# Layer 2's value and output projections as seven products of halves, the output projection in pieces between the next tile's attention steps

## The chip, the cores and the metric

The kernel runs on one core of one Trainium2 chip. The metric is the device time of one execution in microseconds (us). Before the change the median of three runs is 2681.82 us (2680.32 to 2683.97). Times inside an execution come from one profiled execution, whose span is 2682.0 us.

## What is computed

A trunk of two layers over x, 2048 positions of 1024 channels, in float32. Layer 1 is a gated mixer; its output plus x is the residual stream `x1`. Layer 2 is attention over the own chunk of 64 positions and the eight before it:

```python
k, v = jnp.split(rms_norm(x, g_kv) @ w_kv, 2, axis=-1)      # 16 heads of 64
q, z = jnp.split(rms_norm(x, b_norm_g) @ w_qz, 2, axis=-1)
sc = einsum('bqhd,bkhd->bhqk', q * scale, kc) + rel_bias    # 576 keys for each chunk
o  = einsum('bhqk,bkhd->bqhd', softmax(sc), vc)
x  = x + (o * silu(z)) @ w_out
return rms_norm(x, final_g)
```

Every float32 product is made as three products of rounded parts: high x high, high x low, low x high (`mm3`, lines 105 to 108). The low part is what is left of a number after rounding; so each matrix that enters a product is first split, by a copy on ACT (ScalarE) and a subtraction on DVE (VectorE).

## The kernel before

Layer 1 (lines 230 to 957) takes the first half of the time. It already computes its big products block by block as seven products of half-size matrices in place of eight (phases in the order 1, 2, 6, 5, 7, 4, 3, line 499), with sums and differences of quarter matrices on both sides and of the results. Its last stage, called `Po`, is its output projection; it leaves x1 in DRAM and the first 512 rows normalized and transposed in SBUF.

Layer 2 goes over four tiles `t` of 512 positions, and in each tile over eight pairs `p` of heads. For a pair:

- `project(t, p)` (line 988) multiplies the transposed, split input (`xT[t]`) by the weights of Q and of K (`one`, line 975: 24 matmuls of 512 columns each, named `pj`) and, for every second pair, by those of V for two pairs (`proj_v`: four blocks of 128 positions, 24 matmuls of 256 columns each, named `vp`). K and V are split and kept in DRAM for the next tile, which sees this tile's keys as its past.
- `gate(t, p)` makes z of a pair: 24 more `pj` matmuls.
- eight steps `u`: `score` (matmuls `s`; then maximum on DVE, exp on ACT, scaling on POOL, that is GpSimd, line 1135), `flip` (transposes `tp`, a copy on ACT and a subtraction on DVE), and `value` (matmuls `pv`). The scores are two steps ahead of the flips. `value` ends with `og`, the gated output of the pair, kept in SBUF.

While a pair's eight steps run, the next pair's projections are taken in pieces from a generator (`ahead`, `share`, `take`), so that matmuls of the projections fill the waits of attention. In tile 0 each weight block (512 KB) is loaded, scaled by the norm's gain on POOL (line 183), stored as one block (`wk`, `wvv`) and split; in the later tiles the scaled block is loaded again and split again (`load_split`, line 192).

After the last pair of a tile, `b4` (line 1215) does the output projection, `bo`: 192 matmuls of 512 columns, with attention of the next tile only at its end (two scores). Weights are loaded and split there, `og` is split there, the residual is added from DRAM and the final norm is put off to the next tile's steps (`finals`). In the last tile, `b4` is cut in pieces (`tail`) that run beside the last pair.

Transfers are issued from SP, in the order in which its queue has them, and an issue waits in that queue until its data or its buffer is ready. Weight halves lie in eight buffers of 4 KB per partition (tag `T`), fresh blocks in four (tag `raw`). The order of the instructions of each engine is fixed ahead of time: the program's order is their priority, and one that waits by the compiler's plan is passed by later ones.

Of the kernel before, what the change touches and what calls it, by code (L numbers as in the profile page):

```python
# [33 lines left out]
def trunk_kernel(  # L34
# [25 lines left out]
    wk3 = [dram.tile([P, 3, KD * P], F32, name=f"wk3_{p}") for p in range(NPAIR)]  # L60
    wvv = [dram.tile([P, 2, 1024], F32, name=f"wvv{p}") for p in range(NPAIR // 2)]
# [4 lines left out]
    vhd = [  # L66
        [dram.tile([4, P, T], F32, name=f"vhd{t}_{p}") for p in range(NPAIR // 2)]
        for t in range(NT - 1)
    ]


# [38 lines left out]
    def inv_rms(src, name):  # L110

        st = sm.tile([P, 2, 6], F32, tag="st", name=f"st_{name}", bufs=4)
        for c in range(2):
            nc.vector.bn_stats(st[:, c, :], src[:, c * 512 : (c + 1) * 512])
        return inv_rms_of(st, name)

    def inv_rms_of(st, name):
        mv = sm.tile([P, 2], F32, tag="mv", name=f"mv_{name}", bufs=4)
        nc.vector.bn_aggr(mv[:], st[:])
        r = sm.tile([P, 1], F32, tag="rr", name=f"rr_{name}", bufs=4)  # L120
        nc.vector.scalar_tensor_tensor(
            r[:], mv[:, 0:1], mv[:, 0:1], mv[:, 1:2], op0=ALU.mult, op1=ALU.add
        )
        nc.vector.tensor_scalar(r[:], r[:], EPS, None, op0=ALU.add)
        nc.gpsimd.tensor_tensor(r[:], r[:], mhalf[:], op=ALU.pow)
        return r

    def norm_transpose(name, src, pool, tag, bufs, banks=None, junk=None):

        th = sh.tile([P, KD, T], F32R, tag="hh", name=f"hh_{name}")  # L130
        tl = sh.tile([P, KD, T], F32R, tag="hl", name=f"hl_{name}")

        xs = {}

        def norm(b):
            xt = pool.tile([P, D], F32, tag=tag, name=f"bx_{name}_{b}", bufs=bufs)
            nc.sync.dma_start(xt[:], src(b))
            if junk:
                r = sm.tile([P, 1], F32, tag="rr", name=f"rr_{name}_{b}", bufs=4)
                nc.scalar.activation(  # L140
                    junk(f"jk_{name}_{b}"), xt[:], AF.Square, scale=1.0 / 32, accum_out=r[:]
                )
                nc.vector.tensor_scalar(r[:], r[:], EPS, None, op0=ALU.add)
                nc.gpsimd.tensor_tensor(r[:], r[:], mhalf[:], op=ALU.pow)
# [1300 lines left out]
```

## Time and profile before

| what | value |
|---|---|
| median of three runs | 2681.82 us |
| profiled execution, span | 2682.0 us |
| PE busy | 2647.9 us, 99% |
| DVE, ACT, POOL busy | 1920.2, 1275.1, 710.7 us |
| transfers | 615.10 MB on SP's queue, 66.0% of 16 engines' span |
| layer 2 begins at | 1349 us |

The profile names an instruction by its line, its engine, and what it writes and reads (`vp<-wh_bv,hh_b`: the value projection from the high halves of a weight and of the input). PE is the matrix engine, PEld its weight loads, which run beside the matmuls. Busy times of PE count matmuls that overlap in its pipeline. A row of stretches has the stretch, its length, each engine's busy time with its count of instructions, PE's granted clock, the share of the 16 DMA engines that was busy, and GB/s.

### The profile page before, as it was taken

Reading aid. Unit: us, or ns where it says so; the run is one execution under the profiler, and the core shown is the slowest. Engines: PE = TensorE matmul, PEld = TensorE weight load, DVE = VectorE, ACT = ScalarE, POOL = GpSimd, SP = SyncE. Lnnn points to the kernel's source line nnn. Section 1 sums busy time; section 2 is a strip of 40 time slices with the busy share of each in tenths; the row PEclk is TensorE's granted clock in tenths of the full one; section 3 lists DMA queues with packets and bytes.
Section 4 is the critical chain, followed back from the end, with each engine's and each line's share of the span. In section 5 each row is a group of like instructions: output and inputs, shape, how many; then the busy total and the mean of one; then the engine's idle time right before and its main releaser. Section 6 shows DMA issues by size and latency. Waiting matters only on the chain.

```text
span 2682.0 us, 39989 instructions
## 1 busy us (share of the span) xinstructions
PE 2647.9 (99%) x14176; PEld 2272.3 (85%) x14176; DVE 1920.2 (72%) x3187; ACT 1275.1 (48%) x2252; POOL 710.7 (26%) x767
## 2 busy tenths in 40 slices
PE   8999999999999999999999999999999999999997
PEld 7888888888888888888888888888988889888996
DVE  5655677766677568667667666877878777787777
ACT  5422242443434334323255554566655666556663
POOL 3511335152252414014044520211202111021110
PEclk9999999999999999999999999999999999999998
DMA  7898998989888868758476654554455444454331
GB/s 295 316 329 329 345 362 328 328 305 354 328 317 282 313 245 323 279 199 309 152 273 204 203 187 157 181 158 144 158 157 182 146 148 158 142 161 122 115 111 65
DMA packets 212070, 617.65 MB, mean 230 GB/s; under 512 B 24608, under 2 KB 24608, under 8 KB 211872
## 3 DMA queue, kind: packets, MB, share of 16 engines
q1 hardware_dynamic: 211872, 615.10, 66.0%
q8 instruction: 113, 1.85, 0.3%
q14 instruction: 85, 0.70, 0.1%
HBM read 468.21 MB, written 136.31 MB: 225 GB/s over the span
## 4 chain that ended last, share of the span: by engine, by line
PE 90%; DVE 5%; DMA 1%; POOL 1%; issue 1%; ACT 1%; SPq 0%; DVEq 0%; POOLq 0%; ACTq 0%
PE P L108 11%; PE P L107 11%; PE P L106 11%; PE pj L106 6%; PE pj L107 6%; PE pj L108 6%; PE s L1116 4%; PE tp L1155 4%; PE Po L108 4%; PE Po L106 4%; PE Po L107 4%; PE pv L1182 4%; PE vp L108 2%; PE vp L106 2%; PE vp L107 2%; PE bo L106 2%
## 5 line engine op out<-in xcount | busy, mean ns | idle before, releaser
L106 PE MATMUL P<-T,S 128*128 128x512 f32 x1248 | 496.0, 397 | 2.1 <-ACT S L280 2.1
L107 PE MATMUL P<-T,S 128*128 128x512 f32 x1248 | 489.2, 392 | 1.1 <-DVE T L283 1.1
L108 PE MATMUL P<-T,S 128*128 128x512 f32 x1248 | 490.1, 393 | 0.0
L1135 POOL TENSOR_SCALAR pr<-pr,sl 128x640 f32<-128x640 f32 (+4 forms) x256 | 202.2, 790 | 759.2 <-DVE sl L1134 666.4
L1131 ACT ACTIVATE pr<-pr,nm 128x640 f32<-128x640 f32 (+4 forms) x256 | 195.5, 764 | 266.3 <-DVE nm L1124 263.6
L106 PE MATMUL pj<-hh_b,wh_b 128*128 128x512 f32 x768 | 312.0, 406 | 0.2 <-ACT hh_b L166 0.2
L107 PE MATMUL pj<-hl_b,wh_b 128*128 128x512 f32 x768 | 302.7, 394 | 0.0
L108 PE MATMUL pj<-hh_b,wl_b 128*128 128x512 f32 x768 | 301.6, 393 | 0.0
L108 PEld LDWEIGHTS P<-T,S 128*128 128x128 f32 x1248 | 235.4, 189 | 50.3
L106 PEld LDWEIGHTS P<-T,S 128*128 128x128 f32 x1248 | 235.8, 189 | 47.0 <-ACT S L280 2.3
L107 PEld LDWEIGHTS P<-T,S 128*128 128x128 f32 x1248 | 235.7, 189 | 47.0 <-DVE T L283 1.3
L1159 DVE TENSOR_TENSOR pt<-tp,pt 128x640 fp32r<-128x640 f32 (+4 forms) x256 | 188.8, 737 | 59.1 <-ACT pt L1158 56.5
L1124 DVE CUSTOM_DVE_ANT_0 pr<-s,bias 128x640 f32<-128x640 f32 (+4 forms) x256 | 188.2, 735 | 46.4 <-PE s L1116 42.6
L108 PEld LDWEIGHTS pj<-hh_b,wl_b 128*128 128x128 f32 x768 | 144.5, 188 | 33.3
L1155 PE MATMUL tp<-ident,pr 128*128 128x128 f32 x1120 | 165.0, 273 | 6.2 <-DVE pt L1159 5.0
L1158 ACT CAST pt<-tp 128x640 fp32r<-128x640 f32 (+4 forms) x256 | 159.2, 622 | 22.3 <-PE tp L1155 17.8
L1155 PEld LDWEIGHTS tp<-ident,pr 128*128 128x128 f32 x1120 | 134.7, 140 | 33.9 <-POOL pt L1148 4.8
L106 PEld LDWEIGHTS pj<-hh_b,wh_b 128*128 128x128 f32 x768 | 144.9, 189 | 19.2 <-ACT hh_b L166 0.5
L107 PEld LDWEIGHTS pj<-hl_b,wh_b 128*128 128x128 f32 x768 | 145.3, 189 | 17.4
L106 PE MATMUL vp<-wh_bv,hh_b 128*128 128x256 f32 x512 | 148.8, 291 | 0.9 <-ACT hh_b L166 0.9
L108 PE MATMUL vp<-wh_bv,hl_b 128*128 128x256 f32 x512 | 146.0, 285 | 0.2
L107 PE MATMUL vp<-wl_bv,hh_b 128*128 128x256 f32 x512 | 145.5, 284 | 0.0
(212 smaller groups left out, 6027.3 us busy)
## 6 DMA issues: line engine op xcount, KB each, us to landing
S<-hsd SPq DMA_DIRECT2D x288, 512.0 KB, 5.4
rw<-in_w_a SPq DMA_DIRECT2D x108, 512.0 KB, 6.2
raw_b<-wk SPq DMA_DIRECT2D x75, 512.0 KB, 3.6
A<-ytd SPq DMA_DIRECT2D x72, 512.0 KB, 5.2
hsd<-S SPq DMA_DIRECT2D x56, 512.0 KB, 4.0
bias<-reld SPq DMA_DIRECT2D x64, 320.0 KB, 3.4
raw_bo<-in_wb_out SPq DMA_DIRECT2D x36, 512.0 KB, 4.1
va<-vd SPq DMA_DIRECT2D x32, 512.0 KB, 5.2
```

The source lines that it names most:

```text
L106: mm(ps, lh, rh, start=first, stop=False)
L107: mm(ps, lh, rl, start=False, stop=False)
L108: mm(ps, ll, rh, start=False, stop=last)
L1116: mm(ps[:, sg, :w], q[:, qb * P : (qb + 1) * P], kx[:, koff + sg * w : koff + (sg + 1) * w], start=i == 0, stop=i == 1,)
L1124: nc.vector.tensor_tensor_reduce(out=pr[:, c0:].rearrange("p (a b) -> p a b", a=nseg), in0=ps[:, :nseg, :w], in1=bias[:, c0:].rearrange("p ...
L1131: nc.scalar.activation(pr[:, c0:], pr[:, c0:], AF.Exp, scale=-1.0, bias=nm[:], accum_out=sl[:])
L1135: nc.gpsimd.tensor_scalar(pr[:, c0:], pr[:, c0:], sl[:], 1.0, op0=ALU.mult, op1=ALU.mult)
L1155: tpose(tp[:, b, :], pr[:, b * P : (b + 1) * P], ident[:])
L1158: nc.scalar.copy(oh, tp[:, b0:5, :])
L1159: nc.vector.tensor_tensor(pt[:, 1, b0 + qq : 5 + qq, cs], tp[:, b0:5, :], oh.bitcast(F32), op=ALU.subtract)
L1182: mm(po[:, 0, :], keys(i), pt[:, j, i, :], start=(t == 0 and j == 0 and i == blocks[0]), stop=(j == 1 and i == blocks[-1]),)
```

## The change

Four things are changed, all in layer 2 or in what prepares it.

1. **Values.** The whole value projection of a tile is done at once (`v_all`) as seven products of halves: rows in blocks of 128 (even and odd blocks are the two halves), the inner dimension in two halves of 512, the columns in two halves of 512. Each product is 2 x 4 x 3 = 24 matmuls of 512 columns. The weights' sums (`v_sums`) are made in layer 1's last stage and kept in DRAM (`vwf`); in tile 0 they are loaded, split, and both halves stored (`vws`); later tiles load the halves. The sums of the input run on POOL. The results are split and stored in DRAM, and `values` loads, for each pair, the keys' values of the last and of this tile.
2. **Outputs.** The gated output goes to DRAM (`ogd`). `o_all(t)` is the output projection in the same form, with weight sums made beside pairs 1 to 4 of tile 0 (`o_sums`). It runs in pieces of three matmuls beside tile t + 1's attention, by the table `SHARE`; the last tile's runs partly beside its last pair and then to the end. The finished rows go to DRAM (`x2d`) and come back for the final norm; the sums of squares are made on ACT.
3. **Weights of Q, K and z.** Tile 0 splits them and stores both halves (two stores of 512 KB in place of one); later tiles load the two halves and don't split.
4. **Order.** The next tile's norm, transposes, first projections and values stand beside the last pair of a tile (76 steps), and its first two scores are issued there too. With V done at once, `gate` is run for each pair.

The core of the diff:

```diff
+    def split_w(raw, name, keep):
+        wh, wl = w_tile(f"wh_{name}"), w_tile(f"wl_{name}")
         nc.scalar.copy(wh[:], raw[:])
         nc.vector.tensor_tensor(wl[:], raw[:], wh[:].bitcast(F32), op=ALU.subtract)
+        for i, w in enumerate((wh, wl)):
+            nc.sync.dma_start(keep[:, i, :], w[:].bitcast(F32))
         return wh, wl
+    def kept_w(keep, name):
+        out = [w_tile(f"w{i}_{name}") for i in "hl"]
+        for i, w in enumerate(out):
+            nc.sync.dma_start(w[:].bitcast(F32), keep[:, i, :])
+        return out
+    def v_right(t):
+        def right(ph):
+            out = []
+            for q in range(2):
+                name = f"bv{t}_{ph}_{q}"
+                if t:
+                    out.append(kept_w(vws[ph, q], name))
+                    continue
+                raw = sh.tile([P, 1024], F32, tag="T", name=f"raw_{name}", bufs=8)
+                nc.sync.dma_start(raw[:], vwf[ph, q][:])
+                out.append(split_w(raw, name, vws[ph, q]))
+            return out
+        return right
...
+        def values(t, p):
+            v = vtl[t, p] = sb.tile([P, 8, 256], F32R, tag="V", name=f"V{t}_{p}", bufs=2)
+            for i, tt in enumerate((t - 1, t)):
+                if tt >= 0:
+                    nc.sync.dma_start(v[:, i * TB : (i + 1) * TB, :].bitcast(F32), vhd[tt][:, p])
...
+        PHS = (1, 7, 2, 6, 5, 4, 3)
+        def strassen(name, right, left, evict):
+            for ph in PHS:
+                rt = right(ph)
+                lt = left(ph)
+                for jp in range(2):
+                    views = lt(jp)
+                    ps = pmm.tile([P, 512], F32, tag="mm", name=f"{name}_{ph}_{jp}")
+                    for k in range(4):
+                        hi, lo = rt[k // 2]
+                        c = slice((k % 2) * 512, (k % 2) * 512 + 512)
+                        mm3(ps[:], *views[k], hi[:, c], lo[:, c], k == 0, k == 3)
+                        if k < 3:
+                            yield
+                    evict(ph, jp, ps[:])
+                    yield
...
+            def left(ph):
+                if ph == 1:
+                    for jp in range(2):
+                        a11, a12, a21, a22 = (raw(jp, r, h) for r in range(2) for h in range(2))
+                        tg(a22, a21, a22, op=add)
+                        tg(a21, a11, a21, op=sub)
+                        tg(a11, a22, a11, op=sub)
+                        tg(a12, a12, a11, op=sub)
...
+        def o_sums(u):
+            q, i = divmod(u, 2)
+            cs = slice(i * 512, i * 512 + 512)
+            w = {}
+            for rc in ((0, 0), (0, 1), (1, 1), (1, 0)):
+                w[rc] = c_tile(f"wo{u}_{rc[0]}{rc[1]}")
+                nc.sync.dma_start(w[rc][:], wb_out[rc[0], rc[1], q][:, cs])
+            def keep(ph, src):
+                hi, lo = (half_tile("S", f"so{u}_{ph}{x_}", 6, F32R) for x_ in "hl")
+                nc.scalar.copy(hi[:], src)
+                tv(lo[:], src, hi[:].bitcast(F32), op=sub)
+                for n, y_ in enumerate((hi, lo)):
+                    nc.sync.dma_start(ows[ph, q][:, n, cs], y_[:].bitcast(F32))
...
-                ogt[t, p] = og
+                o4 = og[:].rearrange("p (j r s) -> p r j s", j=2, r=2)
+                for r_ in range(2):
+                    nc.sync.dma_start(ogd[t][:, r_, p], o4[:, r_])
...
+        SHARE = {1: (0, 9, 9, 9, 9, 10, 10, 0), 2: (0, 9, 9, 9, 9, 10, 10, 0)}
+        SHARE[3] = (0, 3, 4, 4, 4, 4, 4, 33)
...
         def ahead(t, p):
             if p + 1 < NPAIR:
                 yield from project(t, p + 1)
+                values(t, p + 1)
+                if p == 0:
+                    yield from gate(t, 0)
+                yield from gate(t, p + 1)
             elif t + 1 < NT:
-                yield from project(t + 1, 0, b1(t + 1, sb, "bx", 2))
-            else:
-                yield from tail
+                norm, block = b1(t + 1, bank4, junk)
+                for b in range(TB):
+                    norm(b)
+                for b in range(TB):
+                    block(b)
+                    yield
+                yield from project(t + 1, 0)
+                yield from v_all(t + 1)
+                values(t + 1, 0)
+            if t:
+                yield from some(outs[t - 1], SHARE[t][p])
+            if t + 1 == NT and p + 1 == NPAIR:
+                yield from some(outs[t], 16)
```

`w_tile` is a buffer of the eight with tag `T`. `tg` is a sum on POOL, `tv` one on DVE.

646 lines of the change are left out of this document (361 added, 285 removed).

## The prediction

> **What bounds the kernel now.** I read the page's busy shares first, then the stretches by tile of layer 2, then the transfers.
>
> ```profile
> span 2682.0 us, 39989 instructions
> PE 2647.9 (99%) x14176; PEld 2272.3 (85%) x14176; DVE 1920.2 (72%) x3187; ACT 1275.1 (48%) x2252; POOL 710.7 (26%) x767
> ...
> q1 hardware_dynamic: 211872, 615.10, 66.0%
> ```
>
> The matrix engine is busy 99% of the span, so at first sight every matmul taken away is time won. The profiled span of 2682.0 us and the median of the runs, 2681.82 us, are the same to 0.01%, so I sum against the span and add nothing for what lies around it. The transfers move 615.10 MB in 66.0% of the span: 347 GB/s for each full share of the 16 engines. That second row is what the change leans on. Five stretches say more: one of layer 1 in which the transfers are full, then the four tiles of layer 2 (columns: length; busy time of PE, PEld, DVE, ACT and POOL; clock; share of the DMA engines; GB/s).
>
> ```profile
> 325.00:375.00 50.00, 50.00 (x233) 41.79 (x232) 36.38 (x57) 19.62 (x32) 11.64 (x8) 1.00 1.02 406
> 1349.00:1669.00 320.00, 312.45 (x1800) 273.02 (x1801) 217.17 (x488) 170.56 (x382) 113.59 (x164) 0.98 0.63 210
> 1669.00:2009.00 340.00, 338.76 (x2081) 301.72 (x2080) 270.18 (x525) 202.44 (x361) 64.42 (x104) 1.00 0.51 158
> 2009.00:2349.00 340.00, 338.57 (x2081) 301.50 (x2080) 269.98 (x525) 202.26 (x361) 64.46 (x104) 1.00 0.49 154
> 2349.00:2682.00 333.00, 318.87 (x1916) 281.55 (x1914) 260.26 (x509) 191.06 (x343) 63.12 (x99) 0.98 0.37 116
> ```
>
> The most that the transfers carry for long is 406 GB/s, with a share of 1.02, and PE lost nothing under it. Tile 0 of layer 2 moves 210 GB/s over 320 us, which is 67.2 MB; tiles 1 and 2 move 53 MB each. So before the change PE is the bound in every tile, and DVE, at 270 of 340 us, is the next engine.
>
> **PE's part of the change.** A busy time of PE counts overlapping instructions, so I take the distance between starts. The first pair of rows bounds 33 steps of the value projection (256 columns each), the second 18 steps of the output projection (512 columns).
>
> ```profile
> 1365.20 0.28 PE L108 MATMUL vp<-wh_bv,hl_b 128*128 128x256 f32 x1
> ...
> 1369.14 0.28 PE L108 MATMUL vp<-wh_bv,hl_b 128*128 128x256 f32 x1
> ```
>
> ```profile
> 1647.81 0.39 PE L106 MATMUL bo<-wh_bo,oh 128*128 128x512 f32 x1
> ...
> 1651.88 0.39 PE L106 MATMUL bo<-wh_bo,oh 128*128 128x512 f32 x1
> ```
>
> That is 3.94/33 = 0.119 us for a narrow matmul and 4.07/18 = 0.226 us for a wide one. The counts come from the stretches of the value projection (PE's count is the first one in brackets), those of the Q, K and gate projections in tiles 0 and 1, and the groups of the output projection.
>
> ```profile
> 1349.00:1669.00 320.00, 65.97 (x480) 61.93 (x480) 11.43 (x40) 10.43 (x40) 0.98 0.63 210
> 1669.00:2009.00 340.00, 53.01 (x384) 48.76 (x384) 8.91 (x32) 8.40 (x32) 1.00 0.51 158
> 2009.00:2349.00 340.00, 53.01 (x384) 48.77 (x384) 8.90 (x32) 8.39 (x32) 1.00 0.49 154
> 2349.00:2682.00 333.00, 38.88 (x288) 36.45 (x288) 6.79 (x24) 6.35 (x24) 0.98 0.37 116
> ```
>
> ```profile
> 1349.00:1669.00 320.00, 162.94 (x624) 112.68 (x624) 30.01 (x44) 25.78 (x44) 0.98 0.63 210
> 1669.00:2009.00 340.00, 150.79 (x576) 102.94 (x576) 27.45 (x40) 23.41 (x40) 1.00 0.51 158
> ```
>
> ```profile
> L106 PE MATMUL bo<-wh_bo,oh 128*128 128x512 f32 x256 | 101.3, 396 | 3.1 <-ACT oh L1232 3.1
> L107 PE MATMUL bo<-wl_bo,oh 128*128 128x512 f32 x256 | 100.9, 394 | 0.0
> L108 PE MATMUL bo<-wh_bo,ol 128*128 128x512 f32 x256 | 100.8, 395 | 0.7 <-DVE ol L1233 0.7
> ```
>
> Values: 480+384+384+288 = 1536 narrow matmuls, 183 us. Seven products of halves need, per tile, 7 x 2 row pairs x 4 blocks x 3 terms = 168 wide ones; four tiles 672, 152 us. Outputs: 768 wide ones, 174 us, become 672, 152 us. So the arithmetic is worth 31 + 22 = 53 us (2.0%), and no more: the value projection is not cut to 7/8 of wide work but gains also from its width.
>
> By tile (320, 340, 340, 333 us now): tile 0 loses 480 narrow (57 us) and 192 wide (43 us), and gets two value projections, its own and tile 1's, 336 wide (76 us): 296 us of PE work. Tiles 1 and 2 lose 46 and 43 and get 38 for the next tile's values and 38 for the last tile's outputs: 327 us each. Tile 3 loses 34 and 43 and gets two output projections, 76: 332 us.
>
> **The transfers' part.** The split weights are now kept as two halves, high and low, and each product has its own weight blocks. The sizes:
>
> ```profile
> bias<-reld SPq DMA_DIRECT2D x64, 320.0 KB, 3.4
> ...
> raw_bv<-wvv SPq DMA_DIRECT2D x26, 512.0 KB, 3.7
> raw_b<-in_w_kqz SPq DMA_DIRECT2D x24, 512.0 KB, 4.6
> wk<-raw_b SPq DMA_DIRECT2D x24, 512.0 KB, 2.9
> khd<-K SPq DMA_DIRECT2D x48, 256.0 KB, 3.9
> vhd<-V SPq DMA_DIRECT2D x48, 256.0 KB, 2.8
> ...
> Qh<-Qh SPq DMA_DIRECT2D x64, 128.0 KB, 2.2
> ```
>
> A 512 KB block is 0.524 MB. Tile 0 after the change, in order, beside PE's work (0.226 us a matmul; attention is what tile 0 keeps besides, (296 - 76 - 624 x 0.226)/8 = 9.9 us a pair of heads):
>
> a) First projections and the whole value projection. Two weights, each loaded once and stored twice: 3.1 MB. Fourteen value blocks loaded and 28 stored: 22.0 MB. Values stored 4.2 MB, small ones (K, Q copies, bias) 1.7 MB. Together 31 MB; PE has 216 matmuls and two scores, 51 us.
>
> b) Pair 0: four weights of 1.57 MB and 2.5 MB for K, Q, bias, values and the gated output: 8.8 MB against 32 us of PE.
>
> c) Pairs 1 to 4: three weights (4.7 MB), 2.5 MB as before, and a quarter of the output weights' sums, 1.05 MB in and 3.67 MB out: 11.9 MB each against 26 us (72 matmuls and attention). Four: 47.6 MB, 104 us.
>
> d) Pairs 5 and 6: 7.2 MB each against 26 us.
>
> e) Pair 7, with tile 1's values: 28 kept blocks 14.7 MB, two kept weights 2.1, values stored and reread 5.2, x 2.1, small ones 2.5: 26.6 MB against 59 us.
>
> That is 128 MB, nearly double the 67.2 MB of now; PE's 296 us would need 430 GB/s, above the 406 of the fullest stretch. In a, c and e the transfers end last. Three ends for the rate: 406 GB/s (that stretch), 347 (the whole run's per full share), and, if the queue never runs empty so that only the tile's total counts, 128/0.406 = 315 us. Loads here wait for one of eight weight buffers, which stay taken until the stores out of them have landed, so the queue will not always be full; a, c and e are nevertheless nearest to the full stretch. I take 385 GB/s: a 81, b 32, c 124, d 52, e 69, together **358 us, +38**. At 406 it is 76+32+117+52+66 = 343 (+23); at 347 it is 89+32+137+52+77 = 387 (+67).
>
> The Trainium skill, page "DMA: Bandwidth & Descriptors", section Specifications, puts the HBM limit of a core at about 358 GB/s and the fabric's ceiling at 435. By the first, tile 0 would take 378 us and the kernel about 2735 us, by the second 326 and 2683. The 406 GB/s over 50 us above already exceeds the first figure, so I don't use it.
>
> The issuing queue is no end of its own: an issue takes about a third of a microsecond,
>
> ```profile
> 1354.93 0.32 SPq L189 DMA_DIRECT2D wk<-raw_b  x1
> ```
>
> and tile 0 has some 300, about 100 us of 358. But it works in order, so a store that waits for its split holds the loads issued behind it. What else is moved, the next tile's first two scores out of the old output projection into the last pair, keeps its count and lies beside the values' matmuls: 0, and about 2 us if the pair is already waiting, which is inside the bounds below.
>
> **Tiles 1 to 3.** There the 24 weights come as ready halves, so 24 splits each leave ACT and DVE; DVE falls below its 270 us although the new sums and evictions come in, and is no bound. A tile moves about 100 MB: 53 now, 12.6 more for halves, 10 more each for value and output weights, the rest for values read by pair, the gated output's and the residual's round trips. Over 327 us that is 306 GB/s. Only the last pair is short: 26.6 MB, 69 us, against 48.8 + (327 - 76 - 130)/8 = 64 us of PE. With 2 us for the four norm blocks which now stand at that pair's head, tiles 1 and 2 take 334 us: **-6 each**. Bounds -13 (all hidden) and 0 (at 347 GB/s).
>
> Tile 3 has no value projection. The output's last products now need the gated output back from DRAM:
>
> ```profile
> 2636.89 0.70 DVE og L1206
> 2637.62 0.52 ACT oh L1232
> 2638.18 0.80 PE bo L106
> 2638.98 0.43 PE bo L107
> ```
>
> Now PE goes on 1.3 us after the gated output is begun. After, a store (2.8 us in the row of vhd) and a load (3.7 in that of wvv) stand between, 6.5 us, and nothing else is left to do. Bounds: 0, if the two early products of that tile are still running, and 10, if the clock stays low longer. -1 for PE and +6.5: **+5**.
>
> The extra value-weight sums in layer 1's last stage (about 9 MB more transfers over 300 us, beside matmuls) I put at +2, between 0 and 6. The sums on POOL (0.26 busy on the page) lie beside matmuls; without that cover they would delay the scaling of the scores, which stands behind them in POOL's queue.
>
> Sum: 38 - 6 - 6 + 5 + 2 = +33 us, 2682 + 33 = 2715 us.
>
> **Rivals.**
>
> *The transfers are hidden.* If loads run ahead far enough that tile 0 is limited only by its total (315 us, -5) and tiles 1 and 2 take PE's time (-13 each), tile 3 at +5 and layer 1 at 0, the result is 2656 us; at 343 us for tile 0 and -13, -13, +5 it is 2684. For it speaks the full stretch of layer 1, with PE busy for 50.00 of 50 us. Against it, eight buffers shared by loads, splits and stores. The point of decision is tile 0's time: with tiles 1 and 2 at -13 each the kernel is faster below 341 us, with them at -6 below 325. Chance 0.22.
>
> *Late transfers stall the in-order engines.* In tile 0 POOL scales a fresh weight as soon as it lands, and the score's scaling queues behind it:
>
> ```profile
> POOL raw_b L183 <- DMA raw_b<-in_w_kqz: 157.6, 15, 66.9
> ```
>
> Today those waits cost little; with a full queue they push back the scores and so PE. PE's clock then falls: the last of the four rows above, a matmul that follows a wait, has 0.43 us against 0.226. Tile 0 at 347 GB/s (+67), some 5 us of low clock, tiles 1 and 2 at 0, tile 3 and layer 1 at +10: about 2764 us. Chance 0.23. The Trainium skill, "TensorE: Matmul & The Clock Gate", Part 1, says that an idle window of about 3.4 us halves the clock; the 0.43 agrees, and the 5 us above hold it already.
>
> *The change doesn't do what it says:* the sums cost PE or DVE what the products save, so that even without full transfers nothing is won. Against it: the sums run on POOL, and DVE and ACT lose more splits than they gain. The time would be 2682. Chance 0.05.
>
> The forecast itself, 2690 to 2745, has 0.50.
>
> **From this the numbers.** 2715 us; range 2660 to 2764, from hidden transfers to the stalled case. What this measurement can tell from no change is about 0.2%, 5 us. Faster than that 0.20, within it 0.09 (the weak end of the first rival and the third), slower 0.71.
>
> **What would show it.** In the profile after: value and output projections with 672 matmuls each; tile 0 of layer 2 longer than 340 us with a DMA share above 0.9 and PE idle in its first 80 us and in pairs 1 to 4; tiles 1 and 2 shorter than 340; a wait of some 6 us near the end. I am wrong if tile 0 takes under 330 us, if its rate passes 406 GB/s, or if PE's idle time there waits on splits or scores rather than on transfers.

## The result: 9% slower, and the profile after

| | before | after |
|---|---|---|
| median | 2682.27 us (2680.32 to 2683.97, four runs) | 2925.04 us (2920.11 to 2930.84, four runs) |
| profiled span | 2682.0 us | 2924.7 us |
| layer 2 begins at | 1349 us | 1348 us |

The ratio is 1.0903, with a 95% interval of 1.0888 to 1.0919. The forecast was 2715 us in a range of 2660 to 2764: the sign was right, the size 210 us off.

The page of the kernel after, with the lines that answer to those of before:

```profile
span 2924.7 us, 38938 instructions
...
PE 2698.2 (92%) x13216; PEld 2237.6 (77%) x13216; DVE 1845.4 (63%) x3009; ACT 1246.8 (43%) x2274; POOL 888.1 (30%) x903
...
q1 hardware_dynamic: 302160, 831.67, 82.0%
```

There are 960 matmuls fewer, and PE's share has fallen from 99% to 92%. Its busy time is nevertheless 50 us longer: the matmuls became slower. Layer 2 by stretches (columns as in the prediction: length; busy time of PE, PEld, DVE, ACT, POOL; clock; share of the DMA engines; GB/s). The first two are tile 0, cut where its value projection ends; the others end where the next tile's value projection ends, and the last is tile 3.

```profile
1348.00:1482.00 134.00, 85.10 (x244) 55.94 (x245) 52.81 (x86) 41.48 (x73) 27.87 (x31) 0.77 0.78 271
1482.00:1825.00 343.00, 279.44 (x1265) 223.09 (x1264) 189.49 (x427) 158.15 (x357) 119.61 (x164) 0.88 0.80 271
1825.00:2186.00 361.00, 334.88 (x1825) 284.16 (x1824) 232.63 (x455) 180.83 (x346) 101.33 (x130) 0.98 0.84 276
2186.00:2543.00 357.00, 334.46 (x1843) 284.83 (x1842) 234.95 (x463) 182.45 (x350) 102.07 (x132) 0.99 0.86 280
2543.00:2925.00 382.00, 326.11 (x1743) 275.87 (x1741) 226.56 (x441) 166.11 (x321) 106.82 (x132) 0.92 0.72 238
```

Set beside the forecast:

| part | forecast | measured | missed by |
|---|---|---|---|
| layer 1 ends | 1351 | 1348 | -3 |
| tile 0, first stretch (a) | 81 | 134 | +53 |
| tile 0, the rest (b to e) | 277 | 343 | +66 |
| tile 1 | 334 | 361 | +27 |
| tile 2 | 334 | 357 | +23 |
| tile 3 | 338 | 382 | +44 |
| sum | 2715 | 2925 | +210 |

In tile 0 the two rows move 36 and 93 MB: 129, and 128 were forecast. So not the amount was wrong but the rate, 271 GB/s, and that with a fifth of the DMA engines' time unused. The reader is to see two signs together there: a share of 0.78 to 0.80, and a PE clock of 0.77 and 0.88. Neither PE nor the DMA engines are full, so each of them waits for something.

What it is in the first stretch, SP's queue shows. The rows are its issues during the value projection of tile 0, and one of ACT beside them:

```profile
1399.62 0.50 SPq L205 DMA_DIRECT2D raw_bv<-vwf  x1
1406.13 0.32 SPq L176 DMA_DIRECT2D vws<-wh_bv  x1
1407.39 0.32 SPq L176 DMA_DIRECT2D vws<-wl_bv  x1
1407.80 0.40 SPq L205 DMA_DIRECT2D raw_bv<-vwf  x1
```

```profile
1405.06 1.04 ACT L173 CAST wh_bv<-raw_bv 128x1024 fp32r<-128x1024 f32 x1 [7.14 <-DMA raw_bv<-vwf]
```

A load is issued at 1399.62 and the next one 8.2 us later, at 1407.80, behind the two stores (1406.13 and 1407.39) of the block that the first load brought. Those stores wait in the queue until that block has landed and is split: ACT sat idle for 7.14 us until it landed. So one fresh block at a time is under way: load, split, store, next load. Fourteen blocks of about 8.2 us are 115 us, and the value projection took from 1367 to 1482, for 168 x 0.226 = 38 us of PE. Its clock went down with it:

```profile
1400.00:1475.00 75.00, 44.73 (x104) 28.65 (x102) 23.73 (x34) 15.22 (x25) 15.07 (x8) 0.68 0.79 273
```

### The profile page after: what moved, and what is told of

It reads as the page before. It is cut to its first block, busy times and chain, and to the rows that moved or that the text cites. A ratio compares the mean times of both kernels' runs of the same rounds, so it can differ in the third digit from the quotient of the medians.

```text
span 2924.7 us, 38938 instructions
## 1 busy us (share of the span) xinstructions
PE 2698.2 (92%) x13216; PEld 2237.6 (77%) x13216; DVE 1845.4 (63%) x3009; ACT 1246.8 (43%) x2274; POOL 888.1 (30%) x903
## 5 line engine op out<-in xcount | busy, mean ns | idle before, releaser
L116 PE MATMUL pj<-hh_b,wh_b 128*128 128x512 f32 x768 | 317.9, 414 | 33.2 <-ACT wh_b L173 27.4
L118 PE MATMUL pj<-hh_b,wl_b 128*128 128x512 f32 x768 | 309.5, 403 | 12.9 <-DMA wl_b<-wks 12.5
L117 PE MATMUL pj<-hl_b,wh_b 128*128 128x512 f32 x768 | 308.7, 402 | 0.9 <-DVE hl_b L155 0.9
L1254 PE MATMUL s<-K,Qh 128*128 128x320 f32 (+1 forms) x448 | 118.3, 333 | 38.6 <-DVE nm L1262 29.2
L1321 PE MATMUL pv<-pt,V 128*128 128x256 f32 x960 | 144.9, 293 | 0.0
L1254 PEld LDWEIGHTS s<-K,Qh 128*128 128x128 f32 x448 | 84.3, 193 | 66.9 <-DVE nm L1262 39.0
```

The source lines that it names most:

```text
L116: mm(ps, lh, rh, start=first, stop=False)
L117: mm(ps, lh, rl, start=False, stop=False)
L118: mm(ps, ll, rh, start=False, stop=last)
L1254: mm(ps[:, sg, :w], q[:, qb * P : (qb + 1) * P], kx[:, koff + sg * w : koff + (sg + 1) * w], start=i == 0, stop=i == 1,)
L1321: mm(po[:, 0, :], keys(i), pt[:, j, i, :], start=(t == 0 and j == 0 and i == blocks[0]), stop=(j == 1 and i == blocks[-1]),)
```

## The experiments

Each was run once, with a profile, beside the kernel before on the same chip (2684.24 us for e1 to e4, 2689.34 for e5 to e8, 2682.06 for e9 to e12, 2691.73 for f1 to f4, 2683.17 for g1 and g2). Four runs of the changed kernel lie within 0.2% of their median, 6 us, so I read nothing smaller in a total, and compare by tiles. Tiles that an edit doesn't touch came out up to 7 us away from the changed kernel's. Tile times are in the order of the five rows above: 134, 343, 361, 357, 382 us for the changed kernel (the cuts are at whole microseconds; 1 us either way means nothing). Layer 2 began between 1348 and 1355 us in these runs, which is not the edits' doing.

My theory after the result was that transfers bind tile 0 through what they wait for, and tiles 1 to 3 through the eight weight buffers; the rivals were that the amount of bytes binds, and that DVE and attention's chains do.

**First group: one part undone at a time.** e1_ahead takes away the serial load alone: values' blocks are loaded two at a time into a buffer that is still free then.

```diff
-                raw = sh.tile([P, 1024], F32, tag="T", name=f"raw_{name}", bufs=8)
-                nc.sync.dma_start(raw[:], vwf[ph, q][:])
-                out.append(split_w(raw, name, vws[ph, q]))
+                if q == 0:
+                    rv = sb.tile([P, 2, 1024], F32, tag="V", name=f"raw_{name}", bufs=2)
+                    for i in range(2):
+                        nc.sync.dma_start(rv[:, i, :], vwf[ph, i][:])
+                out.append(split_w(rv[:, q, :], name, vws[ph, q]))
```

> The fresh value-weight blocks of tile 0 are loaded into the two value buffers, a phase ahead, in place of the eight weight buffers; bytes are the same. The first value projection takes 120 us after the change (1367 to 1487). Queue theory (one fresh block in flight, because its load stands behind the last block's two stores): that stretch falls to 70 to 85 us and the kernel to about 2880 to 2890 us. Volume theory (the bytes set the time): the stretch stays above 110 us and the kernel within 10 us of 2925.

Measured: 2920.94 us; tiles 103, 365, 360, 360, 383. The value projection fell from 115 to 84 us, so the serial chain was real; but the time came back in the pairs of tile 0 (343 to 365), and 9 us of 477 were left, hardly more than untouched tiles differ by. The stretch came out as the queue theory had it, the kernel's time as the volume theory had it. In the pairs the same kind of wait stood: SP waited 57.6 us for the splits of Q, K and z, against 37.5 in the changed kernel.

e2_vraw doesn't store the halves of the value weights and splits the sums anew in each tile; e3_kqzraw does the same for Q, K and z, which are stored once, scaled.

```diff
-                if t:
-                    out.append(kept_w(vws[ph, q], name))
-                    continue
                 raw = sh.tile([P, 1024], F32, tag="T", name=f"raw_{name}", bufs=8)
                 nc.sync.dma_start(raw[:], vwf[ph, q][:])
-                out.append(split_w(raw, name, vws[ph, q]))
+                out.append(split_w(raw, name))
```

> The halves of the value weights aren't stored; each tile loads the sums and splits them: 14.7 MB less in tile 0, 7.3 MB less for each later tile. Queue theory: the first value projection falls to about 60 us, the later ones change by under 5 us each, kernel 2855 to 2870 us. Volume theory at the 285 GB/s of the run: 52 us less in tile 0 and 26 us less for each of the three later projections, kernel about 2795 us.

> Weights of Q, K and z as before the change: one store of the scaled block in tile 0, loaded and split again later. 12 MB less in tile 0 and in each later tile, 72 splits more on ACT and DVE. Queue theory: pairs 0 to 6 of tile 0 fall from 270 us to near PE's 208 us because no load waits behind a split's stores, later tiles by under 10 us each, kernel about 2860 us. Volume theory: 42 us less in each of the four tiles, kernel about 2760 us.

Measured: e2_vraw 2929.7 us; 97, 340, 382, 369, 388: tile 0 wins 40 us, and tiles 1 to 3 lose 21, 12 and 6, probably since a fresh block and its two halves take three of the eight buffers at once. e3_kqzraw 2905.47 us; 136, 302, 365, 367, 384: with 15 MB less, tile 0 wins 39 us, and tiles 1 to 3, with 12 MB less each, win nothing. In neither run did the kernel's time fit one of the two theories. e5_oraw, the same for the output weights,

```diff
-            return [kept_w(ows[ph, q], f"bo{t}_{ph}_{q}") for q in range(2)]
+                raw = sh.tile([P, 1024], F32, tag="T", name=f"raw_{name}", bufs=8)
+                nc.sync.dma_start(raw[:], ows[ph, q][:, 0, :])
+                out.append(split_w(raw, name))
...
+                nc.sync.dma_start(ows[ph, q][:, 0, cs], src)
```

> Sums of the output weights are stored once as they are and split in each later tile, in place of halves: 7.3 MB less in tile 0 (pairs 1 to 4) and for each of the four output projections. Volume theory (tile 0 costs about 2.5 us for each MB, as the 14 MB of e3 gave 38 us): tile 0 falls from 476 to about 458 us, later tiles by under 5 us each, kernel about 2900 us. If it is not bytes but where waits stand: under 5 us in tile 0, kernel 2915 to 2930.

gave 2947.09 us; 137, 317, 372, 371, 400: tile 0 wins 23, as the amount of bytes would have it, and the others lose 11, 14 and 18, which it wouldn't. And all three together, with the tail of e4_tail below:

> No halves are stored at all (weights of Q, K, z, value and output sums are stored once and split in each tile), and the third output projection is spread as in e4. Tile 0 moves about 87 MB in place of 129. Volume theory: tile 0 falls to about 476 - 42 x 2.5 = 370 us; tiles 1 and 2 stay at 350 to 365 us as bytes don't bind there, tile 3 at 359; kernel about 2790 us. If buffers and waits bind tile 0 and not bytes: tile 0 above 420 us, kernel above 2840 us.

Measured: 2886.24 us; 102, 281, 383, 382, 386, moving 22, 63, 73, 72, 64 MB. Of the kernels so far, the one with the fewest bytes has the longest tiles 1 and 2. The amount of bytes alone therefore does not set the time of those tiles; the row of its tile 1 shows a share of only 0.61.

```profile
1733.00:2117.00 384.00, 346.80 (x1841) 286.84 (x1839) 291.26 (x515) 231.80 (x404) 108.85 (x132) 0.98 0.61 191
```

In tile 0 the three runs e3, e5 and e6 fit the amount of bytes as well: 94 us for 44 MB in e6, whose expectation put 370 us where 383 came. But they also take away stores that wait for splits, so they can't part the two; g2 below does.

**Buffers or bytes in tiles 1 to 3.** e7_six holds two of the eight weight buffers through layer 2 and changes nothing else.

```diff
+        held = [w_tile(f"held{i}") for i in range(2)]
```

> As the kernel after the change, but two of the eight weight buffers are taken out of use in layer 2; no bytes change. If the transfers' rate is held down by the few buffers (each stays taken from its load to the end of its stores): tile 0 grows by 60 us or more and tiles 1 to 3 by 20 us or more each, kernel above 3040 us. If the rate of the DMA engines binds: under 15 us in all.

Measured: 3052.41 us; 139, 345, 404, 407, 405. Tiles 1 to 3 got 43, 50 and 23 us longer with the same bytes, tile 0 only 7, and not the 60 that had been expected. What SP's queue waited for in tile 1 shows why: the issue of a kept weight's load (L182) waits until PE is done with the buffer, and this grew from 39.0 to 70.0 us. The first two rows are of the changed kernel, the third of e7_six (us in total, times, longest):

```profile
SPq L182 <- PE pj L118: 39.0, 16, 6.6
SPq L1062 <- DVE K L1058: 26.6, 15, 6.3
```

```profile
SPq L182 <- PE pj L118: 70.0, 13, 10.4
```

The last four runs of this line take e7_six and let the products of tiles 1 to 3 use the two held blocks, set to a constant, in place of loaded weights: all of them (f1), or one stream alone (f2 outputs, f3 values, f4 Q, K and z). They leave out the loading of those weights. The edit of f2:

```diff
     def kept_w(keep, name):
+        if name.startswith('bo'):
+            return kept_held
```

> In tiles 1 to 3 no weight is loaded: every product takes its weights from two blocks that are set once and hold a constant, so its output is not the reference's; matmuls, attention, splits, sums and the other transfers are all there, in the same order. Six weight buffers, of which tiles 1 to 3 then need none, so the kernel to compare with is the one of six buffers (tile times 139, 345, 404, 407, 405 us). If the weights' way into the buffers binds tiles 1 to 3, tiles 1 and 2 fall to between 327 and 337 us and tile 3 to about 350 (its tail still waits for the gated output). If attention's chains or the last pair's head (DVE) bind them, they stay above 350, as the changed kernel's 361 and 357. Tile 0 stays within 5 us of 345 up to its last pair's 15 us or less.

> Only the output projection's weights are replaced by the two constant blocks (its output is not the reference's); the Q, K, z and value weights of tiles 1 to 3 are loaded into six buffers. If the two streams of weight blocks that share the buffers in the middle pairs are the trouble, tiles 1 and 2 fall from 404 to 340 or less, nearly as with no weights loaded at all. If the number of buffers for Q, K and z alone binds, they stay above 365.

> Only the value projection's weights of tiles 1 to 3 are replaced by the two constant blocks (its output is not the reference's); the others are loaded into six buffers. The value stretch, 60 us with six buffers, falls to about 40 (168 matmuls of 0.226 us), and tiles 1 and 2 from 404 to about 385, whichever of the two theories holds for the middle pairs; tile 3, which has none, stays at 405. If the value stretch stays above 50, it is not bound by its weights but by the head of the last pair and the input's sums.

> Only the weights of Q, K and z of tiles 1 to 3 are replaced by the two constant blocks (its output is not the reference's); value and output weights are loaded into six buffers. If the two streams that share the buffers are the trouble, tiles 1 and 2 fall from 404 to 345 or less, since a phase of the output takes four buffers and has two to run ahead with. If the output stream alone is bound by its four blocks for each phase, they stay above 360.

| loaded in tiles 1 to 3, six buffers | total | tile 1 | tile 2 | tile 3 |
|---|---|---|---|---|
| everything (e7_six) | 3052.41 | 404 | 407 | 405 |
| no output weights (f2_heldo) | 2899.91 | 359 | 353 | 347 |
| no value weights (f3_heldv) | 3013.95 | 390 | 393 | 406 |
| no Q, K, z weights (f4_heldkqz) | 2900.24 | 348 | 347 | 371 |
| none (f1_heldall) | 2840.56 | 335 | 335 | 347 |

The rows of f1_heldall's tiles 1 to 3, and what PE waited for in its tile 2:

```profile
1822.00:2157.00 335.00, 329.41 (x1841) 284.57 (x1840) 236.57 (x463) 181.96 (x351) 102.47 (x132) 0.99 0.44 136
2157.00:2492.00 335.00, 329.23 (x1842) 284.61 (x1842) 237.02 (x463) 182.32 (x350) 102.64 (x132) 0.99 0.43 134
2492.00:2838.00 346.00, 317.37 (x1764) 273.47 (x1762) 232.51 (x447) 167.49 (x325) 108.01 (x133) 0.96 0.37 112
```

```profile
PE tr_b L147 <- DVE hl_b L155: 2.5, 2, 1.3
PE s L1263 <- DVE nm L1271: 1.9, 2, 1.4
```

The same view of the changed kernel's tile 2 (columns: us in total, times, longest):

```profile
PE pj L118 <- DMA wl_b<-wks: 5.5, 6, 1.7
PE tr_b L147 <- DVE hl_b L155: 4.6, 2, 3.2
PE s L1254 <- DVE nm L1262: 3.7, 3, 2.1
PE vp L117 <- DMA wl_bv<-vws: 3.3, 3, 1.3
PE pj L116 <- DMA wh_b<-wks: 2.6, 3, 2.0
```

Without weight loads tiles 1 and 2 take 335 us, with the same matmuls and attention, and DVE as busy as in the changed kernel. So DVE and attention's chains don't hold the changed kernel at 361 and 357, and the weight loads, with their buffers, their bytes and their place in SP's queue, cost it 26 and 22 us. Taking Q, K and z away won 56 and 60 us of the 69 and 72, the outputs' alone 45 and 54: either one nearly frees the other. For the outputs I had expected 340 or less, or above 365, for Q, K and z 345 or less, or above 360; they came out between, at 347 to 359. So with six buffers it is mainly the two streams together, and neither alone. That each waits for blocks which the other holds is the likely reading, but not shown: a stream that isn't loaded also takes bytes out of the transfers (100 MB a tile become 85 or 74) and issues out of the queue, in which stores stand too (K's, L1062, held it for 26.6 us). No run has more than eight buffers, or other stores of tiles 1 to 3 on another queue. The values' stretch fell from 60 to between 44 and 48 us when its loads went, some 12 to 16 us whether the other loads stayed (f3) or went too (f1), but not to the 38 of its matmuls.

The places at which a block's phases begin are a small part at most. e9_aligned gives each pair one whole phase of the output,

```diff
-        SHARE = {1: (0, 9, 9, 9, 9, 10, 10, 0), 2: (0, 9, 9, 9, 9, 10, 10, 0)}
-        SHARE[3] = (0, 3, 4, 4, 4, 4, 4, 33)
+        SHARE = {t: (8, 8, 8, 8, 8, 8, 8, 0) for t in range(1, NT)}
```

> Only the table SHARE: each of the seven phases of an output projection (8 steps) falls into one pair, pairs 0 to 6, where the kernel after the change has 9 or 10 steps a pair, so that a phase begins at the end of one pair and keeps its four weight buffers through the next pair's projections. Buffer theory (in tiles 1 to 3 the eight weight buffers bind, as e7 says): tiles 1 and 2 fall from 361 and 357 to 340 to 345 us, tile 3 to 350, kernel about 2860 us. If the buffers' number counts but not how long a phase keeps them: tile 3 falls by the 22 us of e4, the others by under 5, kernel about 2900 us.

and got 2894.36 us; 136, 341, 352, 358, 354: 9 us in tile 1, hardly more than untouched tiles differ by, and nothing in tile 2. Most of its gain, 28 us, is in tile 3, which the next run explains.

**The tail.** e4_tail gives tile 3 the table of tiles 1 and 2: `SHARE[3] = (0, 9, 9, 9, 9, 10, 10, 0)`, so that the output projection of tile 2 is done before the last pair and only tile 3's own is left there.

> The third output projection is spread over the last tile's pairs 1 to 6 as in the tiles before, none of it beside the last pair. If the end waits because the last two output projections share four buffers and the last pair: PE's idle time after 2800 us falls by 20 to 30 us, kernel about 2900 us. If the end waits for the bytes of both: no change beyond 5 us, as the bytes are the same.

Measured: 2917.58 us; 134, 344, 363, 361, 359: 23 us less in tile 3 (the total fell by 7 only, as layer 2 began 7 us later). The end of the changed kernel, the part of it in which PE does nothing, and then PE's longest waits in its tile 3 and the longest in the end of e4_tail:

```profile
2800.00:2925.00 125.00, 74.01 (x283) 57.29 (x281) 50.37 (x90) 29.03 (x61) 38.39 (x34) 0.76 0.71 242
2830.00:2840.00 10.00, 0.00 (x0) 0.00 (x0) 2.23 (x3) 0.00 (x0) 0.00 (x0) 0.51 0.88 289
```

```profile
PE bo L116 <- ACT Sho L1106: 28.5, 3, 12.4
PE bo L117 <- DMA wl_bo<-ows: 9.1, 5, 3.1
```

```profile
PE bo L116 <- ACT Sho L1106: 10.7, 1, 10.7
```

Three waits for the gated output's high half, 28.5 us together, became one of 10.7. The second row above lies in the longest of the three: in 10 us without a matmul the granted clock is 0.51. Only the last of the three is the way of the last pair's gated output to DRAM and back, as SP's rows show:

```profile
2835.29 1.00 SPq L1444 DMA_DIRECT2D out<-y  x2
2836.34 0.45 SPq L1361 DMA_DIRECT2D A<-ogd  x1
...
2867.78 0.89 SPq L1350 DMA_DIRECT2D ogd<-og  x2
2871.61 0.84 SPq L1361 DMA_DIRECT2D A<-ogd  x2
```

The load at 2836.34 is the first of tile 3's gated output. It brings pairs 0 to 3, which had been in DRAM for long, but its issue stands in SP's queue behind stores of tile 2's finished rows (`out<-y`), which wait for these rows to come back from DRAM and for DVE. Only the store at 2867.78 is of the last pair; PE goes on at 2876.5, after 11.2 us. The two early waits hang on the weight loads as well: f1_heldall, with the changed kernel's table but no weights to load, has only the last one in its tile 3 (and one of 4.8 us for DVE).

```profile
PE bo L116 <- ACT Sho L1115: 9.0, 1, 9.0
```

**What binds tile 0.** Two runs move the same bytes through the same buffers, and differ from the changed kernel in where the stores of split weights are issued. In g1_late a split block's two stores are issued later on SP's queue; in g2_late_act they are also issued from ACT in place of SP.

```diff
-        for i, w in enumerate((wh, wl)):
-            nc.sync.dma_start(keep[:, i, :], w[:].bitcast(F32))
+        def stores():
+            for i, w in enumerate((wh, wl)):
+                nc.scalar.dma_start(keep[:, i, :], w[:].bitcast(F32))
+        due.append(stores)
...
                 nc.sync.dma_start(raw[:], vwf[ph, q][:])
+                flush_due()
...
+                if k == 5:
+                    flush_due()
```

`flush_due` issues the stores that are due: for values behind the load of the next block, for Q, K and z after six of the block's eight steps. g1_late has `nc.sync` in the place of `nc.scalar`.

> In tile 0 the two stores of a split weight are issued later on SP's queue: for values behind the load of the next block, for Q, K and z after six of the block's eight steps. Bytes and buffers are the changed kernel's. If tile 0 is bound by loads held behind stores in SP's queue, the first stretch falls from 133 to about 105 us and tile 0's total (476 us with its pairs) by 25 or more, and the rate passes 285 GB/s. If tile 0 is bound by what its transfers move at the rate that loads and stores together reach, the first stretch gets shorter and the pairs longer, with the total within 10 of 476.

> As the run with stores issued later, but the split weights' stores of tile 0 are issued from ACT, so that no store of a weight stands before a load in SP's queue; ACT waits for the splits on DVE in their stead. Bytes and buffers are the changed kernel's. If the order in one queue binds tile 0, its total falls from 476 to 430 us or less and the rate passes 300 GB/s. If the amount to be moved binds it, or ACT's waits take the place of SP's, the total stays above 460.

Measured: g1_late 2924.07 us; 104, 355, 361, 364, 387: tile 0 at 459, between the two expectations. Its queue still waited 49.8 us for the splits of Q, K and z, in front of the loads, so the run hardly tested the order in the pairs. g2_late_act 2866.59 us; 106, 299, 365, 360, 382: tile 0 at 405 us, 72 us less, and the rest as in the changed kernel. First the two rows of its tile 0, then what SP waited for most in the changed kernel's pairs, and in its own:

```profile
1353.00:1459.00 106.00, 73.56 (x241) 51.73 (x242) 54.19 (x83) 39.33 (x71) 25.00 (x29) 0.84 0.92 326
1459.00:1758.00 299.00, 258.20 (x1263) 208.15 (x1262) 195.95 (x426) 158.88 (x356) 121.50 (x163) 0.95 0.92 317
```

```profile
SPq L176 <- ACT wh_b L173: 37.5, 11, 6.3
SPq L1350 <- DVE og L1345: 18.3, 6, 3.7
```

```profile
SPq L1083 <- PE pv L1335: 11.1, 4, 6.5
SPq L1074 <- DVE K L1070: 9.3, 6, 3.3
```

The share rises from 0.78 and 0.80 to 0.92 in both parts, with the bytes unchanged (129 MB in both), and PE's clock from 0.77 and 0.88 to 0.84 and 0.95. PE's busy time falls from 85 + 279 = 364 to 74 + 258 = 332 us for the same matmuls at the higher clock; the other 40 of the 72 us are idle time. That a higher clock alone would have won the 32 isn't shown. That having all in the one queue costs tile 0 some 72 us is shown, 18 of which the later place on SP's queue had won already. It is shown for three causes together: a store on ACT's queue holds no load back; SP has fewer issues to make (76 stores, at 0.32 us each about 24 us); and the stores get a DMA queue of their own (q10 in its page, 39.85 MB). Issues alone are too few for 72 us, and the loads did not land sooner with two queues (`raw_b<-in_w_kqz` in tile 0 6.7 us in the median, against 5.3), so the first is the likely main cause. I have no run that parts them.

**Combinations.** None beats the kernel before.

> e1, e3 and e4 together: value-weight blocks loaded ahead, weights of Q, K, z stored once, the third output projection spread. Volume theory: the bytes of e3, so tile 0 as in e3, 438 us, and the tail of e4, kernel about 2880 us. If the waits add up: V(0) 84 us as in e1 and pairs as in e3, tile 0 about 405 us, kernel about 2850 us.

> e9 with e8's other two edits (weights of Q, K, z stored once and split again; first value weights ahead). Buffer theory: e8's 2872 less some 20 us in each of tiles 1 and 2, about 2830 us. Otherwise 2865 to 2875 us.

> e9 with the first value weights ahead, halves kept for all. As e9, within 10 us, if tile 0 only moves its waits as in e1; 30 us less if with e9's order the gain of e1 in the first value projection stays.

> e10 with the output weights' sums stored once and split in each tile. Tile 0 moves 21 MB less than after the change: at the 2.9 us for each MB of e3 and e5 together tile 0 falls to about 400 us and the kernel, with e10's later tiles, to about 2800 us. If the fresh output blocks, which take two more weight buffers at a time, bind the later tiles as in e5: 2830 us or more.

Measured: e8_kqz_ahead_tail 2871.65 us (95, 336, 364, 362, 359), e10_al_kqz_ahead 2846.58 (95, 334, 352, 356, 357), e11_al_ahead 2894.54 (102, 367, 353, 358, 361), e12_al_kqz_ahead_oraw 2865.73 (93, 314, 366, 368, 369). e8's tile 0 (431) lies between its two expectations, and so does e10's total; e11 is as e9; in e12 tiles 1 to 3 grew, as in e5. e10, the best, is still 6.1% above its kernel before. Its edits together with stores from ACT were not tried.

## Why the forecast was wrong, by its own steps

**PE's arithmetic: right.** The two projections have the 672 matmuls each that were counted: three terms of 224 (for the values 128 and 96, which differ in the input that they read).

```profile
L116 PE MATMUL bo<-wh_bo,Sho 128*128 128x512 f32 x224 | 94.8, 426 | 30.6 <-ACT Sho L1106 28.5 <-DMA wh_bo<-ows 2.1
...
L116 PE MATMUL vp<-wh_bv,Shv 128*128 128x512 f32 x128 | 54.2, 448 | 28.2 <-ACT wh_bv L173 22.9 <-DMA wh_bv<-vws 5.3
...
L116 PE MATMUL vp<-wh_bv,hh_b 128*128 128x512 f32 x96 | 39.0, 420 | 12.8 <-ACT wh_bv L173 12.8
```

With no weights to wait for, tiles 1 and 2 took 335 us against the 327 of PE work that the sum had. So of the 13 us a tile that the arithmetic was to save against 340, 5 are left there; the other 8 are the last pair's head (below), and the rest of the forecast's error lies in the transfers and what they wait for.

**Bytes: right. Their rate in tile 0: the step that failed first.** The forecast said that "a, c and e are nevertheless nearest to the full stretch" and took 385 GB/s. Two things are wrong with that. The rate for a full share is 271/0.78 = 347 and 271/0.80 = 339 GB/s here, the low end of the three that were weighed (406/1.02 = 398 was layer 1's); with that, and the queue never empty, tile 0 would have been the 387 us of the upper bound. And the DMA engines stand idle a fifth of the time. I had seen that loads wait for buffers "which stay taken until the stores out of them have landed", and that a store "that waits for its split holds the loads issued behind it", and put the price of both into a rate between 347 and 406 at a full share. Neither is a rate: each is a chain, 8.2 us for a block in the first stretch, and its price is the number of blocks times the chain. e7_six shows that two buffers fewer matter little in tile 0 (+7 us), g2_late_act that the queue in which the stores stand matters most (-72). The queue's own time, which the sum left out, was put too low as well: tile 0 has 337 issues that take 164 us, not some 300 and 100. What remains to the forecast of 358 is 405 - 358 = 47 us: 129 MB at the 347 GB/s of a full share (326/0.92 = 354, 317/0.92 = 345) are 372 us, 14 above the forecast, and the 33 us left are the share of 0.92.

The Trainium skill, page "DMA: Bandwidth & Descriptors", section "Issuing engines are not separate DMA queues", says that issuing from several engines saves only the sequencer's time to issue, which is usually small. For the engines' ceiling the trace agrees: the rate per full share is 339 and 347 GB/s with one queue, 345 and 354 with two. For the time it doesn't: tile 0 went from 477 to 405 us, and the issues saved are only some 24 us. The likely reason is that an issue that waits for its data holds those behind it, which that section doesn't count.

**Tiles 1 and 2: the second failing step.** "A tile moves about 100 MB" was right (100), "tiles 1 and 2 take 334 us" was not. Bytes over time is the wrong measure there: with 12 MB less (e3_kqzraw) they were no shorter, with fewer buffers much longer. The forecast named eight buffers for tile 0 only. Both the 24 weights of a tile and the 14 of the outputs are now in two halves, and a phase of the outputs keeps four of the eight buffers for its 24 matmuls, which are spread over nearly a whole pair; nothing in the sum priced that. Its bounds, -13 to 0, came from rates, so they could not hold +21 and +17. The last pair's head, put at 2 us, is longer too:

```profile
2100.00:2125.00 25.00, 17.83 (x87) 15.86 (x88) 21.67 (x37) 16.48 (x32) 17.47 (x16) 0.80 0.68 234
```

PE is idle for 7 of 25 us there, with DVE at 21.67. That part doesn't go with the weights. In f1_heldall's tile 1, PE is busy all through the pairs before, and then has the same head:

```profile
1822.00:2080.00 258.00, 258.00 (x1481) 224.55 (x1480) 178.54 (x357) 139.44 (x265) 72.51 (x102) 1.00 0.44 136
2080.00:2110.00 30.00, 24.41 (x122) 20.15 (x121) 27.46 (x49) 20.87 (x42) 20.37 (x20) 0.89 0.44 141
```

Its 5.6 us of idle time and the clock of 0.89 (about 3 us of 30, an estimate) make up the 8 us between 327 and f1_heldall's 335. That 335 is near the forecast's 334 is chance: the forecast's 7 us above PE's work were 5 of transfers and 2 of the head.

**Tile 3: right in kind, wrong in size.** A wait for the gated output's way back was foreseen as one of 6.5 us with bounds of 0 and 10. The wait for the last pair's way was 11.2 us (10.7 in e4_tail, 9.0 in f1_heldall), so that term was too small by 3 to 5 us. Not foreseen were the two waits ahead of it, up to 12.4 us, in which tile 3's first gated output was loaded late, behind tile 2's finished rows in SP's queue, plus 9.1 us for weights and a clock of 0.76 over the last 125 us. The table of shares alone is worth 23 us (e4_tail). With that table unchanged, tile 3 takes 346 us without weight loads and 347 without the outputs' alone (f1_heldall, f2_heldo), against 382. The two overlap, since either does away with the early waits, or most of them.

**Layer 1: as good as right.** Its end moved by -1 us in this run, where +2 was put, and it varies by 7 us from run to run.

**The rivals.** *Hidden transfers* is refuted: no tile of layer 2 passed 280 GB/s, and the case asks for 373 (128 MB in 343 us) to 406 in tile 0. *Late transfers stall the in-order engines* had the right direction; its 2764 us priced the stall at 347 GB/s with a full share and 5 us of low clock. The engine that it named was wrong: POOL waited for fresh weights less than before, not more. (The 157.6 us in the forecast are of the whole kernel; tile 0 had 59.7.) The first row is of tile 0 before, the second of its pairs after (us in total, times, longest):

```profile
POOL raw_b L183 <- DMA raw_b<-in_w_kqz: 59.7, 13, 25.5
```

```profile
POOL raw_b L163 <- DMA raw_b<-in_w_kqz: 6.2, 6, 1.9
```

The stall stood in SP's queue and in ACT's splits, as the forecast's own sign against itself had it ("PE's idle time there waits on splits or scores"): PE waited 23.7 us for splits in the pairs of tile 0, in eight pieces.

```profile
PE pj L116 <- ACT wh_b L173: 23.7, 8, 4.7
```

And the clock was under-priced: 5 us of low clock were put, and PE's busy time in tile 0 fell by 32 us when only the place of the stores got better. *The change doesn't do what it says* is out, since the arithmetic was saved.

**What stays open.** Whether in g2_late_act it was the waiting stores, the saved issues or the second DMA queue; why tile 0 has a share of 0.92 and no more then; and how the 26 and 22 us of the weight loads in tiles 1 and 2 part into buffers and the order of SP's queue.

## What to carry to other kernels

Price a stream of blocks by the chain that one block goes through (load, split, store, the buffer's release) and by how many blocks may be under way, before dividing bytes by a rate: here a share of the DMA engines of 0.78 to 0.80 beside an idle PE was the sign that a chain set the pace. When a change makes two streams share the buffers of one, or puts stores that wait for an engine ahead of loads in one queue, count both as new waits, and try the stores on another engine's queue first (here 72 us). An arithmetic saving of 2% is quickly lost in PE's waits: here the same matmuls also ran at a lower clock where they waited more.

## What the runs showed of the hardware that was not expected

- The rate for a full share depends on the stretch: 398 GB/s in the fullest one of layer 1 (406 at 1.02), 339 to 354 in tile 0 of layer 2, where loads and stores of 512 KB are mixed, with one queue or two.
- Short waits lower the clock. Over 75 us of the values' stretch, with PE busy for 44.73, the mean granted clock was 0.68; in 10 us without a matmul it was 0.51. The Trainium skill, "TensorE: Matmul & The Clock Gate", Part 1, has a table of two states, full and half clock, with half after an idle window of about 3.4 us. The 0.51 agrees, and 0.68 is then a mean of the two, full for about a third of the time and half for the rest. But PE need not be idle for all of such a window. In f1_heldall's last-pair head PE was busy for 1.78 of 3.41 us, its idle time lying in waits of 0.7 us at most, and the 6.82 us behind ran at half clock:

```profile
2081.07:2084.48 3.41, 1.78 (x11) 1.21 (x11) 3.11 (x7) 1.74 (x4) 0.55 (x1) 1.00 0.84 276
2084.49:2091.31 6.82, 5.42 (x22) 4.97 (x23) 5.38 (x16) 6.16 (x14) 3.20 (x6) 0.50 0.78 256
```

- Stores that wait for DVE's splits can stand in ACT's order at a gain: with 76 of them issued from ACT, tile 0 was 72 us shorter. (ACT's busy time, 1245.9 against 1246.8 us, doesn't show their cost, as it doesn't count issues.)
